# The order chain over the score products of an attention step, taken away

## The chip, the cores and the metric

The kernel runs on one core of one Trainium2 chip. The metric is the device time of one execution in microseconds (us); lower is better. The core's engines run in parallel, each through its own queue of instructions in order: PE (TensorE, matrix products; its weight loads are listed apart as PEld), DVE (VectorE), ACT (ScalarE), POOL (GpSimd), and SP, which issues DMAs here.

## The reference, cut to what matters

Two layers of a causal decoder over 512 tokens of width 1024. Layer 0 has four differential heads (kind a, with two 64-wide queries and keys each) and four forgetting heads (kind b, 128 wide); layer 1 has eight dilated heads (kind c, 128 wide). Each layer projects, attends, gates, projects back and adds a per-layer embedding. The scores of a differential head are two products that share nothing but the values:

```
def probs(qb, k):
    s = jnp.einsum('bqhd,bkhd->bhqk', qb, k).astype(jnp.float32)
    return jax.nn.softmax(jnp.where(causal, s, -jnp.inf), axis=-1)
w = probs(q1b, k1) - lam * probs(q2b, k2)
return jnp.einsum('bhqk,bkhd->bqhd', w.astype(v.dtype), v)
```

## The kernel before, in words

All matrix products work on 128-row tiles. Operands are split into a high and a low part, and a product is three matmuls that add up in one PSUM bank: high by high, high by low, low by high (`mm3`, lines 178 to 180, for the projections). A projection tile of 128x512 is 24 such matmuls.

The work is laid out in slots (`slot`). In program order a slot holds: deferred work of earlier slots (`run_deferred`: the transposes of queries and keys at line 416, the transposes of the softmax weights at line 518, the products with the values at line 530), then the score steps that `attend` grants from a budget, then the preparation of weights for the next chunk, then the slot's own projection tile.

A head has three score steps (`head_steps`): blocks 0 and 1 together, block 2, block 3, with up to 384, 384 and 512 score columns. `scores` issues a step's products. For kinds b and c a step has one group of all 128 rows and one PSUM bank. For kind a it has two groups: rows 0 to 63 (first query and key) and rows 64 to 127 (second), each with a bank of its own. The banks come from `psS`, which has two. The loops run over blocks, then over the three terms j, then over the groups, the upper rows first (`reversed(groups)`). Block 0 uses unsplit operands at line 448 (each product shows as two matmul instructions); blocks 1 to 3 use the three terms at line 450. On DVE, line 464 then reads the banks, the lower group's first, in an order that is chained by `tc.issue_after(box["min"])`.

The order of instructions on each engine isn't the program's. The whole program is traced, and a scheduler that plays through a timeline draws up each engine's queue when the kernel is built (`tile.TileContext(nc, schedule_with_timeline_sim=True)`); it also gives out the buffers of a pool at that time. `tc.issue_after(ins)` adds an edge for it: what is traced inside the block stands behind `ins` in the same engine's queue, with no wait for `ins` to finish.

Of the kernel before, what the change touches and what calls it, by code (L numbers as in the profile page):

```python
# [47 lines left out]
def trunk_kernel(  # L48
# [32 lines left out]
    def psS():  # L81
        return psum.tile([P, 512], F32, tag="S", bufs=SB, name=nm("ps_"))
# [355 lines left out]
    def scores(qk, qk0, hh, rows, blocks):  # L438

        groups = [(psS(), slice(p0, p0 + pn)) for p0, pn in rows]  # L440
        mm, o = None, 0
        for i in blocks:
            n = P * (i + 1)
            for j, (a, b) in enumerate(((0, 0), (0, 1), (1, 0)) if i else ((0, 0),)):
                for ps, r in reversed(groups):
                    with tc.issue_after(mm) if mm is not None else nullcontext():
                        if i == 0:
                            mm = T.matmul(ps[:, o:o + n], qk0[r, 0, hh], qk0[r, 1, hh], start=True, stop=True).ins
                        else:
                            mm = T.matmul(ps[:, o:o + n], qk[a][r, 0, hh, i * P:(i + 1) * P], qk[b][r, 1, hh, 0:n],  # L450
                                          start=j == 0, stop=j == 2).ins
            o += n
        return [ps for ps, _ in groups]

    def head_steps(kind, hh, qk, qk0, v, vcol, fin, first, extra=None):
# [13 lines left out]
        def step(blocks):  # L469
# [20 lines left out]
            rows = ((0, 64), (64, 64)) if kind == "a" else ((0, P),)  # L490
            tiles = [ptile() for _ in rows]
            pss = scores(qk, qk0, hh, rows, blocks)
            box.pop("min", None)
            sums = [[weights(ps[:, c_], p_[:, c_], b_) for c_, b_ in zip(cols, biases)]
# [550 lines left out]
```

## Time and profile before

| | |
|---|---|
| median of 3 runs | 691.08 us (690.97 to 691.53) |
| the profiled execution | 691.08 us, of which span 689.3 us |
| PE busy | 680.7 us, 99% of the span |
| DVE, ACT, POOL busy | 449.7, 400.0, 203.3 us |
| granted TensorE clock | 1.00 of full speed in every stage |

The span runs from the first to the last profiled instruction; 1.8 us of the execution lie outside it. In a timeline a row stands for one instruction or for a run of equal ones: its start, its duration, engine, source line, operation, output and inputs, the shape and the count. A matmul's shape begins with the rows and columns of the array that it uses: 64*128 is a product of one row group of kind a, 128*128 one over all rows.

### The profile page before, as it was taken

To read this page: it belongs to the slowest core of one execution; us is meant where nothing else is said; L and a number is where in the kernel's file an instruction comes from. 1 tells how busy PE (TensorE), PEld (TensorE's weight loads), DVE (VectorE), ACT (ScalarE), POOL (GpSimd) and SP (SyncE) were. 2 spreads that over 40 slices of the span, in tenths; PEclk is the share of its full clock that TensorE was granted. 3 is DMA by queue.
4 is the path that set the end of the run, shared out by engine and by line. 5 is a ranking of instruction groups with operands and counts; after the bars stand their busy time and mean duration, and the time that the engine had idled before them with its cause. 6 is when DMAs were issued, how large, how long until landed. Compare 5 with 4: busy or idle time off the path is not lost.

```text
span 689.3 us, 10011 instructions
## 1 busy us (share of the span) xinstructions
PE 680.7 (99%) x3449; PEld 567.7 (82%) x3449; DVE 449.7 (65%) x1050; ACT 400.0 (58%) x838; POOL 203.3 (29%) x411
## 2 busy tenths in 40 slices
PE   7999999999999999999999999999999999999997
PEld 7887778778888888888888888888888888888886
DVE  4648798959779793966574486644768665654342
ACT  6737667747558693337675376555658676434220
POOL 3884331110012445401431243313244231800000
PEclk9999999999999999999999999999999999999999
DMA  8533050314142231431431330212303032143111
GB/s 260 159 92 122 5 150 1 88 36 123 35 128 75 71 85 60 132 121 31 122 100 56 121 123 32 93 46 77 97 28 122 17 107 72 51 153 122 47 62 46
DMA packets 43843, 59.74 MB, mean 87 GB/s; under 512 B 6012, under 2 KB 23948, under 8 KB 43792
## 3 DMA queue, kind: packets, MB, share of 16 engines
q1 hardware_dynamic: 43760, 59.09, 27.9%
q8 instruction: 27, 0.44, 0.3%
q14 instruction: 24, 0.20, 0.1%
q10 hardware_dynamic: 32, 0.01, 0.0%
HBM read 56.98 MB, written 2.11 MB: 86 GB/s over the span
## 4 chain that ended last, share of the span: by engine, by line
PE 92%; DVE 2%; DMA 2%; POOL 1%; issue 1%; ACT 0%; SPq 0%; DVEq 0%; POOLq 0%
PE pu L178 12%; PE pu L179 12%; PE pu L180 12%; PE po L530 5%; PE pu_o L178 4%; PE pu_o L179 4%; PE pu_o L180 4%; PE pu_g L178 4%; PE pu_g L179 4%; PE pu_g L180 4%; PE pu_v L178 4%; PE pu_v L179 4%; PE pu_v L180 4%; PE ps L450 4%; PE px L518 2%; PE px L416 2%
## 5 line engine op out<-in xcount | busy, mean ns | idle before, releaser
L148 DVE SCALAR_TENSOR_TENSOR wl<-raw,gcols,wh 128x512 fp32r<-128x512 f32 x128 | 95.3, 778 | 20.9 <-ACT wh L147 20.5
L179 PE MATMUL pu<-wl,ar 128*128 128x512 f32 x256 | 101.9, 398 | 0.0
L178 PE MATMUL pu<-wh,ar 128*128 128x512 f32 x256 | 101.3, 396 | 0.0
L180 PE MATMUL pu<-wh,ar 128*128 128x512 f32 x256 | 100.6, 393 | 0.0
L147 ACT ACTIVATE wh<-raw,gcols 128x512 fp32r<-128x512 f32 x128 | 85.1, 719 | 21.1 <-DMA raw<-in_w_in_even_dram 8.4
L510 POOL TENSOR_SCALAR P<-P,sm 128x128 f32<-128x128 f32 (+3 forms) x48 | 33.2, 698 | 142.0 <-DVE sm L501 110.4
L151 DVE TENSOR_TENSOR wl<-raw,wh 128x1024 fp32r<-128x1024 f32 x36 | 47.6, 1332 | 14.4 <-ACT wh L150 14.0
L178 PEld LDWEIGHTS pu<-wh,ar 128*128 128x128 f32 x256 | 48.1, 188 | 10.3 <-issue 0.7
L180 PEld LDWEIGHTS pu<-wh,ar 128*128 128x128 f32 x256 | 48.1, 188 | 9.8 <-issue 0.6
L179 PEld LDWEIGHTS pu<-wl,ar 128*128 128x128 f32 x256 | 48.1, 188 | 9.4 <-issue 0.2
L179 PE MATMUL pu<-ar,wh 128*128 128x512 f32 x136 | 53.8, 396 | 0.0
L180 PE MATMUL pu<-ar,wl 128*128 128x512 f32 x136 | 53.7, 395 | 0.0
L178 PE MATMUL pu<-ar,wh 128*128 128x512 f32 x136 | 53.5, 393 | 0.0
L150 ACT ACTIVATE ar<-t 128x512 fp32r<-128x512 f32 (+1 forms) x41 | 25.2, 618 | 47.6 <-DVE t L794 26.0
L466 ACT ACTIVATE P<-P,sm 128x128 f32<-128x128 f32 (+2 forms) x80 | 44.3, 557 | 13.3 <-DVE sm L464 13.0
L179 PE MATMUL pu_v<-wl,ar 128*128 128x512 f32 x128 | 50.7, 398 | 0.0
L178 PE MATMUL pu_v<-wh,ar 128*128 128x512 f32 x128 | 50.3, 397 | 0.5 <-DVE t L743 0.5
L180 PE MATMUL pu_v<-wh,ar 128*128 128x512 f32 x128 | 50.7, 399 | 0.0
L150 ACT ACTIVATE wh<-raw 128x1024 fp32r<-128x1024 f32 x36 | 37.7, 1055 | 21.9 <-DMA raw<-in_w_ple_gate_dram 13.0
L179 PE MATMUL pu_o<-ar,wh 128*128 128x512 f32 x128 | 50.0, 392 | 0.0
L180 PE MATMUL pu_o<-ar,wl 128*128 128x512 f32 x128 | 49.8, 393 | 0.0
L178 PE MATMUL pu_o<-ar,wh 128*128 128x512 f32 x128 | 49.7, 395 | 0.0
(246 smaller groups left out, 1602.9 us busy)
## 6 DMA issues: line engine op xcount, KB each, us to landing
raw<-in_w_in_even_dram SPq DMA_DIRECT2D x16, 512.0 KB, 4.5
raw<-in_w_in_even_dram SPq DMA_DIRECT2D x32, 256.0 KB, 3.2
raw<-in_w_ple_gate_dram SPq DMA_DIRECT2D x16, 512.0 KB, 3.7
raw<-in_w_in_odd_dram SPq DMA_DIRECT2D x16, 512.0 KB, 4.4
raw<-in_w_in_odd_dram SPq DMA_DIRECT2D x32, 256.0 KB, 3.1
raw<-in_w_out_even_dram SPq DMA_DIRECT2D x8, 512.0 KB, 4.5
raw<-in_w_out_odd_dram SPq DMA_DIRECT2D x8, 512.0 KB, 5.0
ar<-in_x_dram SPq DMA_DIRECT2D x8, 256.0 KB, 5.0
```

The source lines that it names most:

```text
L147: A.activation(hi, src, AF.Copy, scale=gain)
L148: V.scalar_tensor_tensor(lo, src, gain, hi.bitcast(F32), op0=OP.mult, op1=OP.subtract)
L150: A.activation(hi, src, AF.Copy)
L151: V.tensor_tensor(lo, src, hi.bitcast(F32), op=OP.subtract)
L178: T.matmul(ps, lh, rh, start=first, stop=False)
L179: T.matmul(ps, lh, rl, start=False, stop=False)
L180: T.matmul(ps, ll, rh, start=False, stop=last)
L416: T.transpose(px[:, b, :], raw[:, b * P:(b + 1) * P], ident)
L450: mm = T.matmul(ps[:, o:o + n], qk[a][r, 0, hh, i * P:(i + 1) * P], qk[b][r, 1, hh, 0:n], start=j == 0, stop=j == 2).ins
L466: A.activation(p_, p_, AF.Exp, bias=st_[:, 0:1], scale=-1.0, accum_out=st_[:, 1:2])
L510: G.tensor_scalar(p1[:, c_], p1[:, c_], s1[:, 2:3], 0.0, op0=OP.mult, op1=OP.add)
L530: T.matmul(po[:, i * P:(i + 1) * P], v[:, j, vcol:vcol + P], pt[:, b_, :], start=(j == 0), stop=(j == i))
```

## The change

Every product of a step but the first was traced inside `tc.issue_after(mm)` with `mm` the product before it, so that a step's products stood in one written order in PE's queue: upper group, lower group, upper group, and so on. The change replaces that block by an empty one. The products, their operands, their banks and the program order stay; the scheduler is free to place each of them by its own readiness.

```
                 for ps, r in reversed(groups):
-                    with tc.issue_after(mm) if mm is not None else nullcontext():
+                    with nullcontext():
                         if i == 0:
                             mm = T.matmul(ps[:, o:o + n], qk0[r, 0, hh], qk0[r, 1, hh], start=True, stop=True).ins
```

## Rows read from the trace of the kernel before

**Rows 1.** The page's first part: engines with busy time, share and instructions.
```profile
PE 680.7 (99%) x3449; PEld 567.7 (82%) x3449; DVE 449.7 (65%) x1050; ACT 400.0 (58%) x838; POOL 203.3 (29%) x411
```

**Rows 2.** The page's chain that ended last, shares by engine.
```profile
PE 92%; DVE 2%; DMA 2%; POOL 1%; issue 1%; ACT 0%; SPq 0%; DVEq 0%; POOLq 0%
```

**Rows 3.** A stretch of kind a: length, busy PE, PEld, DVE, ACT, POOL, granted clock.
```profile
85.00:150.00 65.00, 65.00 (x342) 49.66 (x341) 54.42 (x166) 43.36 (x106) 13.02 (x21) 1.00 0.26 74
```

**Rows 4.** Line 450, all instructions: duration ns min/median/max, first and last start.
```profile
L450 PE MATMUL ps<-ar,ar x120: 274/339/501, 64.8 to 557.1; 128*128 128x256 f32 x24, 128*128 128x384 f32 x24, 128*128 128x512 f32 x24, 64*128 64x256 f32 x16
...
L450 PEld LDWEIGHTS ps<-ar x60: 182/188/192, 63.6 to 556.4; 128*128 128x128 f32 x36, 64*128 64x128 f32 x24
```

**Rows 5.** PE's timeline, 116.3 to 117.7 us: a step in one piece.
```profile
116.56 0.45 PE L450 MATMUL ps<-ar 64*128 64x384 f32 x2
116.84 0.51 PE L450 MATMUL ps<-ar,ar 64*128 64x384 f32 x4
117.28 0.50 PE L179 MATMUL pu_v<-wl,ar 128*128 128x512 f32 x1
```

**Rows 6.** PE's timeline, 129 to 131.7 us: blocks 0 and 1.
```profile
128.95 0.39 PE L179 MATMUL pu_v<-wl,ar 128*128 128x512 f32 x1
129.17 0.39 PE L180 MATMUL pu_v<-wh,ar 128*128 128x512 f32 x1
129.49 0.48 PE L448 MATMUL ps<-qk 64*128 64x128 f32 x2
129.91 0.50 PE L178 MATMUL pu_v<-wh,ar 128*128 128x512 f32 x1
130.24 0.40 PE L179 MATMUL pu_v<-wl,ar 128*128 128x512 f32 x1
130.57 0.37 PE L448 MATMUL ps<-qk 64*128 64x128 f32 x1
...
131.34 0.50 PE L180 MATMUL pu_v<-wh,ar 128*128 128x512 f32 x1
```

**Rows 7.** PE's timeline, 136.6 to 139.1 us: block 2.
```profile
136.75 0.44 PE L450 MATMUL ps<-ar 64*128 64x384 f32 x1
137.12 0.50 PE L178 MATMUL pu<-wh,ar 128*128 128x512 f32 x1
...
138.01 0.44 PE L450 MATMUL ps<-ar 64*128 64x384 f32 x1
138.02 0.79 PE L450 MATMUL ps<-ar,ar 64*128 64x384 f32 x4
138.74 0.50 PE L178 MATMUL pu<-wh,ar 128*128 128x512 f32 x1
```

**Rows 8.** PE's timeline, 144.0 to 146.1 us: block 3.
```profile
144.06 0.49 PE L450 MATMUL ps<-ar 64*128 64x512 f32 x1
144.48 0.49 PE L178 MATMUL pu<-wh,ar 128*128 128x512 f32 x1
144.91 0.50 PE L450 MATMUL ps<-ar 64*128 64x512 f32 x1
144.91 0.97 PE L450 MATMUL ps<-ar,ar 64*128 64x512 f32 x4
145.81 0.44 PE L518 MATMUL px<-ident,P 128*128 128x128 f32 x2
```

**Rows 9.** PE's timeline, 86 to 88.8 us: blocks 0 and 1, another head.
```profile
86.38 0.48 PE L448 MATMUL ps<-qk 64*128 64x128 f32 x2
86.79 0.50 PE L179 MATMUL pu<-ar,wh 128*128 128x512 f32 x1
87.13 0.38 PE L416 MATMUL px<-ident,t 128*128 128x128 f32 x2
```

**Rows 10.** PE's timeline, 92.7 to 94.95 us: block 2 of that head.
```profile
93.61 0.33 PE L518 MATMUL px<-ident,P 128*128 128x128 f32 x1
```

**Rows 11.** PE's timeline, 98.9 to 101.5 us: block 3 of that head.
```profile
99.69 0.49 PE L530 MATMUL po<-pt,ar 128*128 128x128 f32 x2
```

More of the change, by code (lines that the diff above doesn't have):

```diff
@@ L445, in scores @@
                 for ps, r in reversed(groups):
-                    with tc.issue_after(mm) if mm is not None else nullcontext():
+                    with nullcontext():
                         if i == 0:
```

## The prediction

> **What bounds the kernel now.** I read the page's busy times first: PE is busy for 680.7 of 689.3 us, the next engine for 449.7 [rows 1]. The chain that ended last lies on PE for 92% [rows 2]. A busy PE is not a PE at its peak, so I then looked at the stretch that holds most of kind a's scores: from 85 to 150 us PE has no idle time and its clock is granted in full [rows 3]. Whatever PE spends more or less there moves the end by the same amount, and no engine's wait hides it. So the question is what the order of the score products costs on PE itself, and for that I read PE's timeline step by step.
>
> Two prices come out of it. The first is the pace. Two neighbouring projection matmuls of 512 columns start 0.22 us apart, at 128.95 and 129.17 [rows 6]; I scale by columns (estimates): 0.165 us for 384, 0.11 for 256. A product of block 0 shows as two instructions and takes 0.21: the visit at 129.49 lasts 0.42, of which 0.21 is the overhead that comes next. Two products of different row groups share this time: in the step at 116.56 six 384-column products take 0.72 us [rows 5], where six lone ones would take 0.99.
>
> The second is the visit: each time PE goes from 128-row work to 64-row products and back. The last projection before one starts 0.32 us ahead of it instead of 0.22, at 129.17 [rows 6], so entry costs 0.10. Inside, 0.72 us for three pairs of 0.165 leaves 0.22 [rows 5]. The projection behind it holds PE for 0.33 instead of 0.22 (129.91 to 130.24) [rows 6], 0.11 more. A visit costs 0.10 + 0.22 + 0.11 = 0.43 us beside its products, about two 512-column units. The second visits agree: 0.73 us for three units of 0.165 from 138.01 on [rows 7], 0.90 for three of 0.22 from 144.91 on [rows 8], that is 0.23 and 0.24 left.
>
> **The change part by part.** It adds and removes no instruction, no byte, no DMA, and no wait that an engine sees; it removes edges that fixed the issue order. What it can change is which product stands where in PE's queue.
>
> Kinds b and c: one group, one bank. The three terms of a block add up in one place and stay in order; blocks follow by program order. I cost them at nothing. The bound from either side is that the scheduler slips another matmul between or closes such a gap, and the nearest row is entry or exit, 0.1 us each.
>
> Kind a, 12 steps, counted here in order of time. In the trace the two groups of a step start together in six of them (1 to 3 and 7 to 9), as at 116.56 [rows 5]: both banks were free, the written order is also that of the program, and without the chain the earliest ready product is still the same one. Nothing.
>
> In the other six the first product of the upper group stands alone, other work follows, and the rest comes in a second visit [rows 6 to 11]. The lower group was waiting for its bank: `psS` has two, and the banks of the step before come free one after the other. The chain held the upper group's second and third product back behind the lower group's first. Without it they may follow at once. What fills the gap now decides:
>
> - 93.61 and 99.69: transposes of weights and value products [rows 10, 11]. They are deferred work, which stands ahead of the scores in program order, so they would still go first, and then the lower group is ready. I take no change: 0.
> - 136.75: the gap holds three projections (137.12 to 138.01, two of them in the elided lines) [rows 7]. The projection of a slot stands behind its scores, so the upper group's two products (0.33) go ahead of it. The gap was longer than two projections (0.44), so a second visit remains. Before: one unit and then three, four in all, because the lower group's products ran beside the upper's. After: three and three. +2 units of 0.165: +0.33 us.
> - 144.06: the gap holds one projection [rows 8]. The second product of the upper group (0.22) takes its place, the bank is then free, and the rest pairs up: five units instead of four, +0.22, but in one visit: -0.43. Sum -0.21.
> - 129.49: two projections [rows 6], a gap between 0.22 and 0.44; three products of 0.11 make 0.33. Whether that closes the gap is even: +0.33 for the lost overlap, -0.43 x 1/2. Sum +0.12.
> - 86.38: one projection and two transposes [rows 9]. The transposes still go first and keep two visits; two of three small products go ahead, and lose their overlap: +0.22.
>
> Sum: 0.33 - 0.21 + 0.12 + 0.22 = +0.46 us. Both ends: if the upper group goes alone in all six, two units are lost in each, 2 x (0.33 + 0.33 + 0.44) = +2.2 us. If the gap closes in all six, each saves a visit and loses one unit: -6 x 0.43 + 2 x (0.11 + 0.165 + 0.22) = -1.6 us.
>
> The profiled execution took 691.08 us, which is also the median: 691.08 + 0.46 = **691.5 us**.
>
> DVE reads the lower group's bank first, in a chain that stays, and the lower group's last product ends no earlier than now; so I expect no gain behind the scores. No stall is removed, so none moves elsewhere.
>
> One rule speaks against the change. Lone products of one row group need their weight loads hidden behind a matmul of the same rows. The rows say that they are: a load takes 188 ns [rows 4], yet projections, which all use the same 128 rows, follow each other every 0.22 us, just the time of their 512 columns [rows 6]. The Trainium skill, "TensorE: Matmul & The Clock Gate", Part 3, "The mechanism", says that a weight load overlaps with matmuls in flight only when its row group differs. By the rows the sum stays +0.46; if that rule held for 64-row products, the 16 products that go alone in four steps would each show their load.
>
> **The rivals.**
>
> *Lone chains break up (slower).* The upper group's products needn't stay together: transposes and value products that stand ahead of them may come between, each time with a visit of 0.43. Place: the six steps. With all overlap lost the time is 691.08 + 2.2 = 693.3; with one more visit in each step as well (6 x 0.43 = 2.6) it is 695.9. For it: at 99.69 a score product stands between value products that come earlier in the program, so the order is no clean one. Against it: the gaps hold only one to three instructions. It decides against the forecast from two extra visits beside +0.46 on, about +1.4 us.
>
> *Loads show (slower).* 16 lone products with a load of 0.188 each [rows 4] are +3.0, with +0.46 about 694.5. This is the page's rule as a mechanism; the pace of the projections speaks against it.
>
> *The gaps close (faster).* The upper group's products displace what lies in the gap, and the lower group follows in the same visit: -1.6 us, 689.5. For it: a visit costs more than a unit. Against it: in two gaps stands earlier work, and one is longer than the products that could fill it. It decides from five gaps closed on.
>
> *The order doesn't change.* If the second product isn't ready until the first has ended, the scheduler fills the gap as it does now: 691.1 us.
>
> **How the numbers follow.** What a measurement of this kernel can tell from no change is 0.2%, 1.4 us. A changed order also shifts everything the scheduler places later; of that no row gives a price but the entry and exit of 0.1 us, and ten such either way are 1 us. Forecast, with a few gaps changed: 0.45, and no change of order: 0.10, both within 0.2%. Lone chains break up: 0.28; loads show: 0.03; both slower. Gaps close, or the later shifts fall that way: 0.14, faster. So 0.14, 0.55, 0.31. The range leaves out the far end of the broken chains and that of the closed gaps with later shifts added: 689.6 to 693.9. The likeliest case alone spans 690.5 to 692.5.
>
> **What would show it.** In PE's timeline, steps 1 to 3 and 7 to 9 of kind a look as before, the scores of kinds b and c stand in the same order, and at 136.75 three upper products follow each other. The count of visits in the six steps should be 11 or 12, where it is 12 now. The time is lost or won before 150 us, so that all later stages are shifted by the same amount; a stage of kind c that is longer by itself would mean that the later shifts decide. The prediction is wrong if pairs that are now whole come apart, if visits multiply, or if PE shows idle time in the stretch, where the banks on the chip would come free later than the scheduler had it.

## The result, and the profile after

The median of five runs is 694.63 us (694.35 to 697.42) against 691.08 (690.45 to 691.53): a ratio of 1.0062 [1.0045, 1.0078]. The change made the kernel slower by 3.6 us, outside the range of the prediction. The profiled execution took 696.32 us with a span of 694.5.

The page after, first part and chain (they answer to [rows 1, 2]):

```profile
PE 683.4 (98%) x3449; PEld 570.2 (82%) x3449; DVE 448.9 (65%) x1050; ACT 398.8 (57%) x838; POOL 206.9 (30%) x411
...
PE 95%; DMA 1%; POOL 1%; DVE 1%; issue 1%; ACT 0%; SPq 0%; DVEq 0%; POOLq 0%
```

The instructions are the same in number. PE's busy time is 2.7 us more and the span 5.2 us more, so PE has also become idle somewhere. The first place to look is the stretch of [rows 3]; its row after (length, busy PE, PEld, DVE, ACT, POOL, granted clock, DMA share, GB/s):

```profile
85.00:150.00 65.00, 65.00 (x344) 50.04 (x343) 54.15 (x165) 41.69 (x105) 12.26 (x21) 1.00 0.25 74
```

Here nothing is lost: no idle time, full clock. The loss must lie elsewhere, and the list of PE's waits says where (total, times, longest, in us):

```profile
PE px L551 <- DVE ar L148: 2.5, 1, 2.5
PE px L214 <- DMA ar<-in_x_dram: 1.5, 1, 1.5
...
PE pu L178 <- ACT t L386: 0.8, 1, 0.8
```

In the kernel before, PE waits neither in front of line 551 nor for line 386. Line 551 is the matmul that takes the mean over a finished head of kind a (`finish_a`); line 386 reads the PSUM bank of a projection. Both waits stand just after kind a, where the first heads of kind b begin. PE's timeline there, after:

```profile
174.15 1.03 PE L416 MATMUL px<-ident,t 128*128 128x128 f32 x8
177.71 0.47 PE L551 MATMUL px<-t,onesr 128*128 128x512 f32 x1 [2.52 <-DVE ar L148]
...
178.25 0.67 PE L416 MATMUL px<-ident,t 128*128 128x128 f32 x4
...
180.83 0.79 PE L178 MATMUL pu<-wh,ar 128*128 128x512 f32 x1 [0.84 <-ACT t L386]
181.42 0.63 PE L179 MATMUL pu<-wl,ar 128*128 128x512 f32 x1
181.85 0.63 PE L180 MATMUL pu<-wh,ar 128*128 128x512 f32 x1
```

The same instructions in the kernel before:

```profile
163.99 0.60 PE L416 MATMUL px<-ident,t 128*128 128x128 f32 x4
...
169.22 0.60 PE L416 MATMUL px<-ident,t 128*128 128x128 f32 x4
...
174.93 0.39 PE L551 MATMUL px<-t,onesr 128*128 128x512 f32 x1
```

Read the counts. A group of four transposes (line 416, queries and keys of one tile) fills one bank of `psX`, which has two. Before, the two groups stand 5.2 us apart and each bank is emptied long before line 551 needs it. After, eight transposes stand back to back: both banks are full at once, and line 551, which takes its bank from the same pool, waits until ACT and DVE have emptied one. The projections behind it stand in PE's queue and wait too. The chain after shows what PE waits for:

```profile
174.31 0.45 PE px L416 x4
174.79 0.48 ACT ar L147
175.30 0.50 DVE ar L148
175.82 0.47 ACT qk L421
176.29 0.37 ACT ar L147
176.69 0.89 DVE ar L148 x2
177.71 0.47 PE px L551
```

Then the clock: after the idle time the projections start 0.43 us apart (181.42, 181.85) where it was 0.23. The windows show it (length, busy PE, granted clock, DMA share, GB/s):

```profile
172.00:176.00 4.00, 3.19 (x19) 1.00 0.02 6
176.00:180.00 4.00, 2.28 (x11) 0.83 0.10 34
180.00:184.00 4.00, 3.17 (x8) 0.50 0.09 32
184.00:188.00 4.00, 4.00 (x16) 0.82 0.01 2
```

0.50 is the 1.2 GHz level. The three windows lack 0.17 + 0.50 + 0.18 of a clock, 0.85 x 4 us = 3.4 us at most, since PE stood idle for part of it. The clock did not fall alike in all five runs: in two its mean over the run is 1.000, and they took 694.35 and 694.63; one of 0.998 took 694.52; the two of 0.994 and 0.995 took 697.42 and 696.32. The traced execution is that of 696.32. If the others wait as it does, which no trace shows, 2.5 + 0.8 us of waits stand in the median, and the clock adds 2 to 3 us in some runs.

How the transposes came together can be read back, though only read, from DVE's timeline. After:

```profile
144.53 0.69 DVE L464 CUSTOM_DVE_ANT_0 P<-ps,causal 128x512 f32<-128x512 f32 x1 [2.36 <-PE ps L450]
...
148.87 0.69 DVE L151 TENSOR_TENSOR t<-sq,t 128x512 fp32r<-128x512 f32 x1
```

and before:

```profile
145.55 0.69 DVE L151 TENSOR_TENSOR t<-sq,t 128x512 fp32r<-128x512 f32 x1 [2.69 <-ACT t L150]
146.16 0.68 DVE L464 CUSTOM_DVE_ANT_0 P<-ps,causal 128x512 f32<-128x512 f32 x1
```

In the new order the last step's minima (line 464) go ahead of the low part of a finished head (line 151). That head's mean on PE moves from 150.20 to 153.19, ACT stands idle for 5.88 us before it goes on at 154.72, the reading of the next projection's bank (line 384) starts at 155.65 instead of 152.82, and the first two normalised tiles (line 411 on DVE) come at 169.40 and 170.66 instead of 159.28 and 163.84. The 2.8 us at line 384 grow to 10 at line 411 on DVE: before, the small steps that lead there (lines 129 to 132) end at 158.98, ahead of the splitting of the next chunk's weights (line 148, from 160.37); after, that splitting starts at 159.34, and the small steps stand among it, from 163.26 to 168.19. The tiles are late and close together, and so are their transposes.

### The profile page after: what moved, and what is told of

Its sections match the earlier page's. It is cut to its first block, busy times and chain, and to the rows that moved or that the text cites. A ratio compares the mean times of both kernels' runs of the same rounds, so it can differ in the third digit from the quotient of the medians.

```text
span 694.5 us, 10009 instructions
## 1 busy us (share of the span) xinstructions
PE 683.4 (98%) x3449; PEld 570.2 (82%) x3449; DVE 448.9 (65%) x1050; ACT 398.8 (57%) x838; POOL 206.9 (30%) x411
## 4 chain that ended last, share of the span: by engine, by line
PE 95%; DMA 1%; POOL 1%; DVE 1%; issue 1%; ACT 0%; SPq 0%; DVEq 0%; POOLq 0%
PE pu L179 13%; PE pu L178 13%; PE pu L180 13%; PE po L530 5%; PE pu_o L180 4%; PE pu_o L178 4%; PE pu_o L179 4%; PE pu_g L180 4%; PE pu_g L178 4%; PE pu_g L179 4%; PE pu_v L179 4%; PE pu_v L180 4%; PE ps L450 4%; PE pu_v L178 4%; PE px L518 3%; PE px L416 2%
## 5 line engine op out<-in xcount | busy, mean ns | idle before, releaser
L180 PE MATMUL pu<-wh,ar 128*128 128x512 f32 x256 | 101.5, 396 | 0.0
```

The costliest lines, as they stand in the source:

```text
L180: T.matmul(ps, ll, rh, start=False, stop=last)
```

## The scores themselves

Taken together, the steps of kind a became better, not worse. The six steps with a gap [rows 6 to 11], after: the tenth and the twelfth are

```profile
129.37 0.50 PE L448 MATMUL ps<-qk 64*128 64x128 f32 x4
129.61 0.37 PE L450 MATMUL ps<-ar 64*128 64x256 f32 x2
129.81 0.40 PE L450 MATMUL ps<-ar,ar 64*128 64x256 f32 x4
130.15 0.50 PE L180 MATMUL pu_v<-wh,ar 128*128 128x512 f32 x1
...
141.97 0.50 PE L450 MATMUL ps<-ar 64*128 64x512 f32 x1
142.31 0.62 PE L450 MATMUL ps<-ar,ar 64*128 64x512 f32 x2
142.86 0.50 PE L178 MATMUL pu<-wh,ar 128*128 128x512 f32 x1
...
143.52 0.50 PE L450 MATMUL ps<-ar 64*128 64x512 f32 x1
143.86 0.63 PE L450 MATMUL ps<-ar,ar 64*128 64x512 f32 x2
```

Five of the six are now one visit (85.72, 91.86, 97.66, 129.37, 135.33); the last is two visits with one group each. Counted in PE's timelines from 50 to 166 us, a visit being a run of `64*128` rows with nothing between, the twelve steps have:

| steps | 1, 2, 3 | 4, 5, 6 | 7, 8, 9 | 10, 11, 12 | all |
|---|---|---|---|---|---|
| before | 3, 2, 1 | 2, 2, 2 | 3, 1, 2 | 2, 2, 2 | 24 |
| after | 3, 2, 1 | 1, 1, 1 | 4, 2, 3 | 1, 1, 2 | 22 |

By the prediction's 0.43 us a visit this is worth 0.9 us. Equal points of the two traces agree with a gain there and a loss behind it. The first score product of kind a starts 0.7 us earlier than before (56.82 against 57.50), the 500th projection matmul 2.1 us earlier (161.23 against 163.31), the 600th 5.0 us later (194.32 against 189.30) and the last 5.2 us later (689.94 against 684.70). The loss of the change is not in the products that it frees. The visits and the waits together make 3.4 - 0.9 = 2.5 us of the median's 3.6; the rest of the median is not accounted for.

## The experiments

Two theories stood after the traces. **The boundary theory**: the score products cost nothing more; the new order shifts the other engines, and at the boundary of kinds a and b both banks of `psX` fill at once, which costs the wait and the clock. **The score theory** (the expectations call it the spread theory): the time goes with the freed steps themselves, each by its own, and the wait only shows it late. The steps of kind a are counted 1 to 12 in order of time; the kernel before ran again beside each group of experiments, at 691.02, 691.16 and 690.85 us. Built with the chain dropped for kinds b and c alone, the queues keep the order of the kernel before, so every experiment is on kind a.

**One step free.** Only step 4 lost its chain; all others keep it.

```
-        mm, o = None, 0
+        mm, o, nstep = None, 0, cnt.append(len(rows)) or cnt[1:].count(2)
...
-                    with nullcontext():
+                    with tc.issue_after(mm) if mm is not None and nstep != 4 else nullcontext():
```

> The chain stays in every step but the fourth of kind a (blocks 0 and 1 of the second head, at 86 us). Boundary theory: the change's loss arises at one place, between 174 and 186 us, where two groups of transposes take both banks of psX ahead of the mean-square product at line 551 and PE idles for some 3.4 us; the fourth step's order alone brings this about. Then the time is 693.5 to 696 us with a wait of the line 551 product of over 2 us, although only one step of six is free. Spread theory: each freed step costs its share, 3.55/6 = 0.6 us, so 691.7 us and no long wait on PE.

Measured: 699.27 us (698.58 to 700.86), ratio 1.0123 [1.0108, 1.0137]. One freed step of twelve costs more than all twelve, 8.3 us, more than either theory gave. PE's timeline of this kernel:

```profile
177.77 1.03 PE L416 MATMUL px<-ident,t 128*128 128x128 f32 x8
181.32 0.64 PE L551 MATMUL px<-t,onesr 128*128 128x512 f32 x1 [2.52 <-DVE ar L148]
```

The same eight transposes, and the same wait to the hundredth. A price by step is ruled out; that the wait is the cause is not shown yet.

**All but one step free.** The chain stays for one step alone: step 4, and, in two later kernels, step 6 and step 5.

```
-                    with nullcontext():
+                    with tc.issue_after(mm) if mm is not None and nstep == 4 else nullcontext():
```

> The reverse: all steps free but the fourth of kind a. Boundary theory: one transpose group comes well ahead of the line 551 product, PE doesn't idle there, and what is left is the effect of the other five freed steps, where gaps close: 689.5 to 691.3 us. Spread theory: five of six shares, +3.0 us, 694.0 us.

Measured: 690.91 us (690.19 to 691.38), ratio 0.9997 [0.9987, 1.0006]. One chain put back removes the whole loss. The two groups of transposes stand at 167.47 and 172.50, and line 551 doesn't wait. What is gained in kind a (21 visits) is given back in a wait of 0.74 for line 386 at 176.92.

> All steps of kind a free but the sixth; the fourth is free here, as in the slow kernels. In this program's order 22 projection matmuls stand between the two transpose groups ahead of the last head's product at line 551. If what costs is those two groups standing back to back right ahead of that product (boundary theory), the long wait at line 551 is gone, and the time is 690 to 692 us. If the free fourth step itself costs (a theory that the first two experiments leave open), it stays at 694 us or above.

Measured: 689.47 us (688.91 to 689.99), ratio 0.9974 [0.9966, 0.9983]: faster than both kernels, and 0.5 us under the boundary theory's range. PE's timeline:

```profile
166.52 0.60 PE L416 MATMUL px<-ident,t 128*128 128x128 f32 x4
...
171.96 0.60 PE L416 MATMUL px<-ident,t 128*128 128x128 f32 x4
...
172.86 0.40 PE L551 MATMUL px<-t,onesr 128*128 128x512 f32 x1
...
174.15 0.39 PE L450 MATMUL ps<-ar 128*128 128x256 f32 x1 [0.45 <-ACT ar L147]
...
175.90 0.50 PE L178 MATMUL pu<-wh,ar 128*128 128x512 f32 x1 [0.69 <-ACT t L386]
```

Apart again, no wait at line 551, two short ones behind it; 18 visits.

> All steps of kind a free but the fifth. In this program's order the two transpose groups stand back to back right ahead of the last head's product at line 551, as in the changed kernel. Boundary theory: a wait of over 2 us on PE between 170 and 190 us and 693.5 to 699 us, although it differs from the fifth run (689.47) only in which of two steps keeps its chain. If the fifth run was fast because fewer steps were free, this one, with as many free, is at 689 to 690.5 us.

Measured: 695.43 us (694.96 to 697.82), ratio 1.0072 [1.0059, 1.0084]. PE's timeline:

```profile
174.72 1.03 PE L416 MATMUL px<-ident,t 128*128 128x128 f32 x8
...
178.27 0.47 PE L551 MATMUL px<-t,onesr 128*128 128x512 f32 x1 [2.52 <-DVE ar L148]
```

Three kernels with eleven free steps each differ by 6 us, and the one whose transposes come together is the slow one, as the boundary theory had it.

**The last two heads free.** The chain stays for steps 1 to 6.

```
+                    with tc.issue_after(mm) if mm is not None and nstep <= 6 else nullcontext():
```

> The chain stays for the first two heads of kind a and is gone for the last two. Boundary theory: no stall at the boundary; the gaps at steps 10 to 12 close or shrink, 0 to -1 us: 690.1 to 691.2 us. Spread theory: half the shares, +1.8 us, 692.9 us.

Measured: 692.04 us (690.69 to 692.32), ratio 1.0010 [1.0001, 1.0019]. Neither theory's number. The transposes stand apart (164.91, 170.17), and line 551 doesn't wait; a wait of 1.16 us for line 386 comes at 178.89, with 23 visits.

**The mean in another bank.** The fourth finished head takes the bank for line 551 from `psO` (the pool of the value products) instead of `psX`. All edges of the change stay dropped.

```
-                pm = psX().rearrange("p a b -> p (a b)")
+                pm = psO() if cnt.append('f') or cnt.count('f') == 4 else psX().rearrange("p a b -> p (a b)")
```

> The changed kernel, all steps free; only the mean-square product of kind a's last head writes the bank of psO, which is idle then, in place of one of psX's two. Boundary theory: the product no longer waits for a bank that the transposes hold; PE's idle time between 160 and 190 us falls from 3.4 to under 1 us, the clock stays in full, and the time is 689.8 to 691.5 us. Spread theory: the freed steps still cost what they cost, 694.6 us.

Measured: 691.84 us (691.29 to 692.47), ratio 1.0012 [1.0003, 1.0021]: 2.8 us less than the change, 0.3 us over the boundary theory's range. The scores' visits are as in the change, 22; the mean now stands at 169.19, before both groups of transposes (174.69, 175.60). Those are still close, with two projections between them, and PE waits behind neither. So the move took away the wait, but it changed the order too: the bank by itself is not separated from that. The window that stood at 0.83 of the clock is full:

```profile
176.00:180.00 4.00, 4.00 (x20) 1.00 0.19 66
```

But another wait, which neither kernel has, comes much later:

```profile
308.31 0.50 PE L178 MATMUL pu_g<-ar,wh 128*128 128x512 f32 x1 [1.15 <-ACT ar L150]
```

The control is the kernel before, chain and all, with the same move:

> The kernel before, chain in place, with the same move of the last head's mean-square product to psO's bank as in the fourth run: its control. The fourth run gave 691.84 with no wait at the boundary but a new one of 1.2 us at a gate projection. If moving the bank is what brings that later wait, this one is at 691.5 to 692.5 us; if the free order brings it, this one is at 690.5 to 691.3 us.

Measured: 690.13 us (lowest 689.77), ratio 0.9989 [0.9981, 0.9998]. That is under both ranges: the move alone gains 1.0 us where there was no wait to remove; with the change it gains 2.8. The later wait for line 150 isn't there, so the move alone doesn't bring it.

**An edge on DVE.** In the change, the minima of line 464 of kind a stand behind the finished head's low part (line 151, here line 547), by an edge on DVE. This was to test whether that exchange alone is what brings the transposes together.

```
-            with tc.issue_after(box["min"]) if "min" in box else nullcontext():
+            with tc.issue_after(box["min"]) if "min" in box else tc.issue_after(st["sqlo"]) if "sqlo" in st and kind == "a" else nullcontext():
...
-            split(hi, lo, sq)
+            A.activation(hi, sq, AF.Copy); st["sqlo"] = V.tensor_tensor(lo, sq, hi.bitcast(F32), op=OP.subtract).ins
```

> The changed kernel, all steps free, with one edge on DVE alone: the minima of a later step of kind a stand behind the low-part subtraction of the head that finished before. In the changed kernel that subtraction had slid behind the twelfth step's minima, from 145.55 to 148.87 us, and line 551's first product behind 29 projections. If the stall at 174 us descends from that (late chain theory), the last head's product no longer waits 2.5 us, and the time is 689.5 to 692 us. If the free order costs on PE itself, it stays near 694.6 us.

Measured: 698.65 us (697.71 to 699.25), ratio 1.0107 [1.0094, 1.0120]. The forecast fell. Line 551 no longer waits, but the transposes are together all the same, and the projections wait instead:

```profile
171.88 1.16 PE L416 MATMUL px<-ident,t 128*128 128x128 f32 x8
176.34 0.50 PE L178 MATMUL pu<-wh,ar 128*128 128x512 f32 x1 [3.30 <-ACT t L386]
```

But the edge did more than put the order of the kernel before back. There the low part, at 145.55, stands between the minima of step 11 (139.02, 139.50) and those of step 12 (146.16). Here it stands ahead of both steps' minima, and DVE's timeline shows what that costs:

```profile
152.93 0.69 DVE L547 TENSOR_TENSOR t<-sq,t 128x512 fp32r<-128x512 f32 x1 [11.65 <-ACT t L547]
153.54 0.55 DVE L464 CUSTOM_DVE_ANT_0 P<-ps,causal 128x384 f32<-128x384 f32 x1
```

The minima of step 11 come at 153.54, where the change has them at 136.94, and the low part itself comes later than in the change (148.87). So this kernel doesn't single out the exchange, and whether the exchange by itself brings the transposes together stays open. It does show a long wait behind two groups back to back where line 551 isn't the product that waits.

**Both together.** One step chained, and the mean in `psO`: first step 4, then step 6.

> The second and the fourth run together: all steps free but the fourth, and the last head's mean-square product in psO's bank. The second run was ahead of the kernel before by some 2 us until 174 us and gave it back at the boundary. If both boundary waits (the bank of psX, and line 178 behind ACT) go with the bank, the gain of the free steps stays: 688.5 to 690 us. If new waits turn up elsewhere, 690 to 692 us.

Measured: 688.32 us (688.31 to 688.97), ratio 0.9961 [0.9950, 0.9973]: 0.2 us under the range of the case without new waits.

> The fifth run with the last head's mean-square product in psO's bank. The fifth run was ahead of the kernel before by some 3 us until 174 us and gave back a little over 1 us at the boundary. If the bank ends that, 687.5 to 688.8 us; if the wait there is another (line 178 behind ACT's copies), 689 to 690 us.

Measured: 686.77 us (686.34 to 687.28), ratio 0.9941 [0.9929, 0.9953]: the fastest of all, 4.1 us under the kernel before and a little under its own forecast. Its page, and PE's timeline at the boundary:

```profile
PE 677.2 (99%) x3449; PEld 566.9 (83%) x3449; DVE 448.0 (65%) x1050; ACT 400.5 (59%) x838; POOL 196.3 (29%) x411
```

```profile
166.13 0.39 PE L551 MATMUL po<-t,onesr 128*128 128x512 f32 x1
...
166.59 0.60 PE L416 MATMUL px<-ident,t 128*128 128x128 f32 x4
...
171.62 0.60 PE L416 MATMUL px<-ident,t 128*128 128x128 f32 x4
```

PE is busy 3.5 us less than in the kernel before [rows 1], with the same instructions.

**All of them in one table.** Visits and waits are from each profiled execution; "waits" are PE's for lines 551, 386 and others that the kernel before doesn't have. The sum is 0.43 x (visits - 24) + waits; beside it stands the profiled execution's time less the median of the kernel before that ran beside it. The last column adds up, over windows of 4 us from 148 to 200, what the granted clock lacks to 1.00, in us.

| kernel | visits | waits, us | sum | measured | clock lost |
|---|---|---|---|---|---|
| the change | 22 | 3.4 | +2.5 | +5.2 | 3.4 |
| only step 4 free | 26 | 4.5 | +5.4 | +7.6 | 1.7 |
| step 4 chained | 21 | 0.9 | -0.4 | -0.7 | 0 |
| last two heads free | 23 | 1.2 | +0.8 | +1.3 | 0 |
| mean in `psO` | 22 | 1.4 | +0.5 | +1.0 | 0 |
| step 6 chained | 18 | 1.1 | -1.5 | -1.3 | 0 |
| edge on DVE | 20 | 4.9 | +3.2 | +7.8 | 3.4 |
| before, mean in `psO` | 24 | 0 | 0 | -1.2 | 0 |
| step 4 chained, `psO` | 21 | 0 | -1.3 | -2.8 | 0 |
| step 5 chained | 23 | 3.0 | +2.6 | +4.5 | 1.7 |
| step 6 chained, `psO` | 18 | 0 | -2.6 | -4.5 | 0 |

The four kernels whose two groups of transposes come back to back are the four with waits of 3 us or more, with a lost clock, and with a time above 694 us. Where the clock held, the sum meets the measured time within 0.5 us, but for three of the `psO` kernels, which gain 1.2 to 1.9 us more; 0.4 of that is the wait for line 510 at line 518 that the kernel before has and these don't, and the rest has no name here. The sum is rough: it leaves out the start, where the wait for the input at line 214 is 0.9 to 2.5 us and the first score product of kind a comes from 0.8 us earlier to 0.1 us later than in the kernel before, and the wait at line 518, which is 0 to 0.8 us. How many steps are free doesn't order the table.

## Why the prediction was wrong

- **The step that failed** is "No stall is removed, so none moves elsewhere", and with it the price of "later shifts": ten entries or exits of 0.1 us, 1 us either way. The shift that came was no entry or exit. It was a wait of 2.5 us and one of 0.8, 30 us behind the last freed product, and on top a lost clock of 2 to 3 us in some runs. The prediction took the order of PE's queue as the only thing that an edge of PE's queue could change; the scheduler redraws DVE's and ACT's too, and gives out the banks anew.
- **The place**: "The time is lost or won before 150 us" is wrong. There PE is fully busy; the loss lies from 174 to 186 us. Its warning that the prediction falls "if PE shows idle time" named the sign, and "the stretch" the wrong stretch.
- **The six steps**: forecast 11 or 12 visits and +0.46 us, measured 7 visits. At 93.61 and 99.69 nothing was to change, and the gaps closed; at 86.38 and 136.75 two visits were to stay, and the gaps closed; at 129.49 it was even, and the gap closed. At 144.06 one visit with five units was forecast, and it is two with three units each. Within the scores the rival "the gaps close" was right, down to its threshold of five, and the unit that it charged for each closed gap hardly came: in steps 5, 6, 10 and 11 all products stand in pairs.
- **Steps 1 to 3 and kinds b and c**: as forecast. **Steps 7 to 9**: forecast unchanged, but they have 9 visits for 6, which gives back three of the five visits won. Pairs that were whole came apart there (in step 9 single products stand at 122.55 and 123.40, where a pair stood at 123.09), one of the prediction's own signs of being wrong. Why, no run shows.
- **A visit's 0.43 us** fits: with it, and with the waits added, four of the seven kernels that kept their clock come out within 0.5 us. The other three, with `psO`, don't, and no run has it by itself. The lone chain of step 12 agrees: 0.89 us from 141.97 to 142.86 for three products of 0.22 and the 0.22 inside a visit.
- **Loads**: that same chain leaves no room for 0.188 a product [rows 4]; its second and third product start 0.23 us apart (142.31, 142.54). "Loads show" was wrong, though its 694.5 is near the median: a number that fits by another cause.
- **The slower rival** "lone chains break up" has the measured time in its span, and not its mechanism: visits fell.

What is shown: the loss lies at the boundary and not in the freed products, and it goes with the two groups of transposes standing back to back, whatever else is free; for steps 5 and 6 this was forecast from the order and came so. Moving the mean to the other bank takes 2.8 us back, of which 1.0 also comes without the change. What is read from traces alone: that the full banks of `psX`, rather than another part of the new order, make line 551 wait; and the way from the freed products over DVE and ACT to the transposes. The experiment on one link of that way, the edge on DVE, changed more than the link. Not tried: bringing the transposes together in the kernel before with all chains in place; and the clock's part was not separated by a run of its own, but only by the spread of the runs.

## What to carry to other kernels

An edge taken out of a scheduled queue changes more than the products it tied: before pricing the edit, look for the places downstream where a pool has just enough banks, because there a small shift turns into a wait of microseconds. Judge such an edit by its parts (which steps lost visits, which waits are new), since the sum can hide a gain: eleven steps freed, one kept chained, and one bank moved gave -4.1 us (the bank alone, -1.0) where the whole change gave +3.6.

## What the runs showed of the hardware

The granted clock fell to its lower level, 0.50, behind some idle times of PE and not behind others. Waits of 1.16 us (at 178.89, with the last two heads free) and 1.15 us (at 308.31, with the mean in `psO`) left it at 1.00. One of 1.38 us at 156.97, in the kernel with the edge on DVE, was followed by 0.50 from 157 to 160. The one of 2.52 us was followed by 0.50 in the traced execution of the change, while two other executions of it kept a mean of 1.000; what they waited is not on record.

Three lone products of one row group ran at the pace of their 512 columns: the second and third start 0.23 us apart (142.31, 142.54), though each has its own weights to load, in 0.188 us (the median of line 450's loads).
